# The first expert's tokens gathered alone, the group's other three behind its first products, and the table of Exp fetched in the projection

## The chip, the cores and the metric

The kernel runs on one NeuronCore of a Trainium2 chip, as one program in one launch. The metric is the device time of that launch in microseconds. Its engines work side by side, each through its own queue in order: TensorE (PE in the profile, with its weight loads listed apart as PEld), VectorE (DVE), ScalarE (ACT), GpSimd (POOL) and SyncE (SP), which here issues nearly all DMA transfers. TensorE's clock has two levels, 1.2 and 2.4 GHz; the profile shows which one was granted (PEclk 0.50 or 1.00).

## What is computed

Two layers of a hybrid backbone over 256 context and 256 latent tokens of 1024 features. In each layer a token mixer with four branches is followed by an expert-choice mixture of experts, and the change lies in the second of these and just ahead of it:

```python
def expert_choice_moe(h, router, w1, w3, w2):
    '''Each expert picks its top-C tokens of the routed set (one sample of one stream) by softmax affinity.'''
    B, L, D = h.shape
    cap = CAPACITY_FACTOR * L // N_EXPERTS
    aff = jax.nn.softmax((h @ router).astype(jnp.float32), axis=-1)
    g, idx = lax.top_k(aff.transpose(0, 2, 1), cap)
    xg = jax.vmap(lambda hb, ib: hb[ib])(h, idx)
    a = jnp.einsum('becd,edf->becf', xg, w1)
    b = jnp.einsum('becd,edf->becf', xg, w3)
    y = jnp.einsum('becf,efd->becd', jax.nn.silu(a) * b, w2) * g[..., None].astype(h.dtype)
    return jax.vmap(lambda yb, ib: jnp.zeros((L, D), h.dtype).at[ib.reshape(-1)].add(yb.reshape(-1, D)))(y, idx)
```

There are 16 experts of inner width 1024, each with three weight matrices of 4 MB in float32. Each expert takes 32 tokens of each stream. `h` is the normalised and modulated residual. Layer 0 routes two streams, context and latent; layer 1 routes the latent stream alone.

## The kernel before

Everything is float32. A float32 product of TensorE shows in the trace as two records, each with a weight load of its own. Time is split into a start, the mixer of layer 0 (to about 644 us), its expert stage (to about 1125), the mixer of layer 1 and its expert stage (from about 1535 to the end).

**The end of the mixer.** The last loop of `mixer` is the output projection: eight column blocks `wo0` to `wo7`, each a weight DMA, a split of the weights on ScalarE (L843) and VectorE (L844), products into a bank called `pd`, and a residual update on VectorE (L1421). After each block `pre.step(d)` of the class `MoePre` squares the new residual on ScalarE (L584) for the sums over tokens; after the last one `tokens` turns these sums, and the router's products, into columns by token.

**The start of the expert stage** (`moe`). VectorE computes a reciprocal root and the logits, ScalarE their Exp (L1454), VectorE the softmax. Then four rounds of maximum, replace and find index pick 32 tokens for each expert and stream (L1469 to L1473). Meanwhile `pre.transposes` turns the residual into rows by token, `xt`, through TensorE (L428) and copies on ScalarE (L674).

**The gather.** The experts go in four groups of four. `one_hot(gr)` builds, for the four experts of a group, a matrix OH of ones at the chosen tokens, scaled by the reciprocal root: one multiply on VectorE (L1571), one product with ones that spreads the rows over the partitions, and a comparison for each stream and half of the tokens (L1577). `gather(gr)` multiplies `xt` with OH, for each of eight feature blocks `k`, stream and half of the tokens one product with 128 x 128 weights out of `xt` and 128 moving columns (4 experts of 32 tokens). A bank `pm` holds two blocks in layer 0 and four in layer 1; there are two such banks in turn, and ScalarE (L1605) and VectorE (L1603) take them out with scale and shift into `xg`, in turns.

**The experts.** `ffn(e)` takes four weight tiles of 1 MB for w1 and four for w3 and multiplies the gathered tokens with them into two banks `pd`; ScalarE's Silu (L1636) and a multiply on VectorE (L1637) give the inner activations, TensorE transposes them (L1640), VectorE copies them (L1641), and the w2 products go into a bank `ps`. The group after next is gathered after the third expert of a group, and `scatter` adds the results to the residual after each group.

**Weights and queues.** A weight tile is fetched by SyncE into a slot (L1614) as soon as the slot's old contents have been read; before the expert stage begins some are already fetched, as slots come free. SyncE issues in order and waits at each slot. The order on the other engines is set by the scheduler from priorities in program order.

## Time and profile before

| | us |
|---|---|
| median of three runs (2004.29 to 2011.41) | 2009.74 |
| the profiled execution's own time | 2006.5 |
| its span in the trace | 2004.7 |
| TensorE busy in the span | 1843.2 (92%) |
| VectorE busy | 854.7 (43%) |
| ScalarE busy | 529.9 (26%) |
| mean DMA rate over the span | 274 GB/s |

A busy share is a mean over stages with different limits. To see what a change in one stage is worth, one goes to that stage: which engine is full there, what the others wait for, and whether a delay there is still seen at the stage's end. The times in the trace count from the start of the span. In the list of waits and in the chain, the line L431 is a helper through which nearly all products go, so one tells them apart by their tiles: `pm` for one-hot and gather, `pd` for the first products of an expert, `ps` for the rest.

### The profile page before, as it was taken

How to read it: one execution, taken by the hardware profiler on the slowest of the kernel's cores; microseconds unless marked ns; L12 is line 12 of the kernel's file. 1: busy time of each engine (PE TensorE's matmuls, PEld its weight loads, DVE VectorE, ACT ScalarE, POOL GpSimd, SP SyncE). 2: the span in 40 equal slices, each digit the busy share in tenths (PEclk: the TensorE clock that was granted, in tenths of full speed). 3: DMA queues.
4: the chain of work that ended last, by engine and by line, in shares of the span. 5: the costliest groups of instructions: out<-in, count | busy, mean ns of one | idle time of the engine just before them, and what ended most of it. 6: DMA issues, size and time to landing. Idle time of an engine off the chain costs nothing.

```text
span 2004.7 us, 28151 instructions
## 1 busy us (share of the span) xinstructions
PE 1843.2 (92%) x11524; PEld 1087.6 (54%) x11524; DVE 854.7 (43%) x1855; ACT 529.9 (26%) x932; POOL 27.9 (1%) x52
## 2 busy tenths in 40 slices
PE   7999999999999899999897799999998999987877
PEld 3667778877887443434232356788997333221213
DVE  5355658798743222221121345869865021110101
ACT  4433447522233110101000243447443000000000
POOL 0000000000000000000000010010000000000000
PEclk9989999999999899999999999999998999999999
DMA  8641122364545999999999855333578999999999
GB/s 312 223 140 58 64 85 78 107 236 136 194 156 218 353 399 350 387 409 409 409 409 409 302 189 180 117 106 137 200 262 336 409 409 409 409 409 409 409 409 332
DMA packets 154148, 550.07 MB, mean 274 GB/s; under 512 B 11042, under 2 KB 22690, under 8 KB 153124
## 3 DMA queue, kind: packets, MB, share of 16 engines
q1 hardware_dynamic: 153444, 545.13, 71.7%
q0 software_dynamic: 576, 3.15, 0.5%
q8 instruction: 91, 1.49, 0.3%
q14 instruction: 37, 0.30, 0.0%
HBM read 545.08 MB, written 3.15 MB: 273 GB/s over the span
## 4 chain that ended last, share of the span: by engine, by line
PE 69%; DMA 19%; DVE 7%; issue 3%; ACT 3%; SPq 0%; DVEq 0%; ACTq 0%
PE pd L431 40%; PE ps L431 15%; DMA base<-moe_w 8%; PE pm L431 7%; DMA r<-moe_w 6%; PE pa L431 4%; DMA base<-ada_w 2%; PE pm L428 1%; DMA base<-wg 1%; DVE base L527 1%; DVE r L844 1%; ACT r L843 1%; PE ps L1640 1%; DMA base<-cb 0%; DVE r L1236 0%
## 5 line engine op out<-in xcount | busy, mean ns | idle before, releaser
L431 PE MATMUL pd<-r 128*128 128x256 f32 (+3 forms) x2976 | 574.4, 364 | 12.9 <-DMA r<-moe_w 6.5
L431 PEld LDWEIGHTS pd<-r 128*128 128x128 f32 (+2 forms) x2976 | 427.3, 184 | 131.4 <-issue 53.8
L431 PE MATMUL pd<-r,r 128*128 128x512 f32 (+3 forms) x1304 | 282.6, 433 | 13.4 <-DMA r<-moe_w 10.8
L431 PEld LDWEIGHTS pd<-r,r 128*128 128x128 f32 (+2 forms) x1304 | 161.8, 166 | 105.0 <-issue 54.8
L844 DVE TENSOR_TENSOR r<-base,r 128x1024 fp32r<-128x1024 f32 x136 | 165.9, 1222 | 110.4 <-ACT r L843 110.0
L843 ACT ACTIVATE r<-base 128x1024 fp32r<-128x1024 f32 x136 | 143.4, 1058 | 252.2 <-PE pd L431 181.2
L431 PE MATMUL ps<-base 32*64 32x64 f32 (+12 forms) x2372 | 177.2, 279 | 15.1 <-DMA base<-hy 5.1
L431 PE MATMUL pd<-r,base 128*32 128x512 f32 (+1 forms) x680 | 166.5, 598 | 11.3 <-DMA r<-moe_w 10.6
L431 PEld LDWEIGHTS ps<-base 32*64 32x64 f32 (+7 forms) x2372 | 112.6, 142 | 76.3 <-issue 42.7
L431 PE MATMUL pm<-base 128*128 128x128 f32 (+12 forms) x660 | 106.1, 327 | 17.5 <-DVE base L1571 5.8
L431 PE MATMUL ps<-r,base 128*64 128x512 f32 (+4 forms) x468 | 98.6, 525 | 12.9 <-DVE base L1641 6.3
L431 PE MATMUL pd<-base 128*32 128x512 f32 (+1 forms) x408 | 100.5, 595 | 6.4 <-DMA base<-moe_w 5.6
L431 PEld LDWEIGHTS pm<-base 128*128 128x128 f32 (+5 forms) x660 | 72.8, 180 | 60.9 <-issue 33.6
L431 PEld LDWEIGHTS pd<-r,base 128*32 128x32 f32 (+1 forms) x680 | 42.0, 122 | 111.2 <-issue 76.4
L1637 DVE TENSOR_TENSOR r<-base,pd 64x512 f32<-64x512 f32 x16 | 10.9, 679 | 214.3 <-PE pd L431 214.3
L1637 DVE TENSOR_TENSOR base<-base,pd 128x512 f32<-128x512 f32 x16 | 11.0, 688 | 190.1 <-PE pd L431 155.9
L1636 ACT ACTIVATE base<-pd 128x512 f32<-128x512 f32 (+1 forms) x32 | 19.0, 594 | 251.1 <-PE pd L431 251.1
L431 PE MATMUL pa<-r,r 128*128 128x512 f32 (+1 forms) x384 | 82.4, 342 | 1.1 <-DVE base L905 1.1
L1687 ACT ACTIVATE base<-ps 32x512 f32<-32x512 f32 (+2 forms) x28 | 14.7, 525 | 251.6 <-PE ps L431 247.2
L1687 ACT ACTIVATE r<-ps 32x512 f32<-32x512 f32 (+2 forms) x32 | 15.3, 480 | 246.2 <-PE ps L431 240.3
L431 PE MATMUL pd<-base,r 128*32 128x512 f32 (+1 forms) x296 | 71.3, 597 | 9.3 <-DMA base<-moe_w 9.3
L1685 DVE COPY r<-ps 32x512 f32<-32x512 f32 (+2 forms) x32 | 17.8, 555 | 123.3 <-ACT r L1687 123.2
(246 smaller groups left out, 1728.8 us busy)
## 6 DMA issues: line engine op xcount, KB each, us to landing
r<-moe_w SPq DMA_DIRECT2D x251, 1024.0 KB, 18.1
base<-moe_w SPq DMA_DIRECT2D x131, 1024.0 KB, 17.4
base<-wg SPq DMA_DIRECT2D x152, 512.0 KB, 3.6
base<-ada_w SPq DMA_DIRECT2D x60, 512.0 KB, 4.7
base<-ada_t SPq DMA_DIRECT2D x24, 512.0 KB, 3.3
r<-ada_w SPq DMA_DIRECT2D x12, 512.0 KB, 10.2
base<-xT SPq DMA_DIRECT2D x4, 1024.0 KB, 6.8
filters<-r SPq DMA_DIRECT2D x8, 256.0 KB, 4.0
```

The costliest lines, as they stand in the source:

```text
L428: T.transpose(out, in_, ident)
L431: return T.matmul(out, lhsT, rhs, start=start, stop=stop, **kw)
L527: V.tensor_tensor_reduce(self.junk() if s == 0 else b(), b(), self.cb(s * 1024, n=1024), 1.0, cs("adab", l * 48 + c * 8 + j, n=1), OP.mult ...
L843: A.activation(w[0](), raw(), AF.Copy)
L844: V.tensor_tensor(w[1](), raw(), F(w[0]()), op=OP.subtract)
L1636: A.activation(s_(np_=rows), pa[0:rows, :], AF.Silu)
L1637: V.tensor_tensor(h_(np_=rows), s_(np_=rows), pb[0:rows, :], op=OP.mult)
L1640: T.transpose(p[:, q * rows:q * rows + rows], h_(q * 128, n=128, np_=rows), cs("ident", n=rows, np_=rows))
L1685: V.tensor_copy(dst, src)
L1687: A.activation(dst, src, AF.Copy)
```

## The change

Three things are changed in both layers.

First, `MoePre.step` issues an Exp of one column after the second block of the output projection, into a buffer that nobody reads.

Second, the first gather of a layer is made by a function of its own, `gather_one`, for expert 0 alone. Its one-hot has 32 columns for each stream and half; its products have 32 moving columns instead of 128 and all lie in one bank. The bank is taken out by VectorE alone, in two halves, by a multiply and an add for each.

Third, the other three experts of the first group are gathered by `gather(0, 1, 3)`, called in `ffn(0)` behind the products of w1 and w3. The one-hot now takes the first expert and the number of experts as arguments. The other three groups are gathered as before.

```diff
--- before.py
+++ after.py
@@ -659,6 +659,10 @@
 
         def step(self, k):
             self.sums.step(k)
+            if k == 1:
+                z = mem.take(8)
+                A.activation(z(n=1), self.sq[1](0, n=1), AF.Exp, scale=-1.0)
+                z.free()
             if k == KB - 1:
                 for b in self.sq + [self.AR]:
                     b.free()
@@ -1566,20 +1570,37 @@
                     else:
                         A.activation(dst, src, AF.Copy)
 
-        def one_hot(gr):
-
-            V.tensor_tensor(ge(0, [[128, NS], [32, 4], [1, 32]], np_=ne), gi(0, [[0, NS], [0, 4], [1, 32]], np_=ne),
-                            cs("sel", gr, [[4, NS], [8, 4], [0, 32]], np_=ne), op=OP.mult)
+        def one_hot(gr, j0, nj):
+
+            n = nj * 32
+            V.tensor_tensor(ge(0, [[n, NS], [32, nj], [1, 32]], np_=ne), gi(0, [[0, NS], [0, nj], [1, 32]], np_=ne),
+                            cs("sel", j0 * 8 + gr, [[4, NS], [8, nj], [0, 32]], np_=ne), op=OP.mult)
             p = ps("m")
-            mm(p[:, 0:NS * 128], cs("ones", np_=ne), ge(n=NS * 128, np_=ne), True, True)
+            mm(p[:, 0:NS * n], cs("ones", np_=ne), ge(n=NS * n, np_=ne), True, True)
             for s in range(NS):
                 for tb in range(2):
-                    V.tensor_scalar(OH((s * 2 + tb) * 128, n=128), p[:, s * 128:s * 128 + 128], cs("tok", tb, n=1),
+                    V.tensor_scalar(OH((s * 2 + tb) * 128 + j0 * 32, n=n), p[:, s * n:s * n + n], cs("tok", tb, n=1),
                                     rs(8 + tb * NS + s, n=1), op0=OP.is_equal, op1=OP.mult)
 
+        def gather_one(gr):
+
+            one_hot(gr, 0, 1)
+            x, p, n = xg[gr % 2], ps("m"), NS * CAP
+            for k in range(KB):
+                for s in range(NS):
+                    c = k * n + s * CAP
+                    for tb in range(2):
+                        mm(p[:, c:c + CAP], pre.xt((s * 2 + tb) * D + k * 128, n=128), OH((s * 2 + tb) * 128, n=CAP),
+                           tb == 0, tb == 1)
+            for k in range(0, KB, 4):
+                dst = x(k * 4 * nt, [[4 * nt, 4], [CAP, NS], [1, CAP]])
+                src = p[:, k * n:(k + 4) * n].rearrange("p (k s c) -> p k s c", s=NS, c=CAP)
+                cols = lambda b, o: b(o + k * 2 + 2 - NS, [[2, 4], [1, NS], [0, CAP]])
+                V.tensor_tensor(dst, src, cols(pre.Ac, 0), op=OP.mult)
+                V.tensor_tensor(dst, dst, cols(mod[l], 48), op=OP.add)
+
         def gather(gr, j0=0, nj=4):
-            if j0 == 0:
-                one_hot(gr)
+            one_hot(gr, j0, nj)
             x = xg[gr % 2]
             n = nj * 32
             per = min(KB, 512 // (NS * n))
@@ -1625,6 +1646,8 @@
                     for half in range(2):
                         mm(p[half * nt:half * nt + nt, :], x((k * 4 + j) * nt, n=nt),
                            w[k // 2]((k % 2) * 1024 + half * 512, n=512), k == 0, k == KB - 1)
+            if e == 0:
+                gather(0, 1, 3)
             read = w1 + w3
             n0 = len(slots)
             for b in read[::-1] if e == 0 else read:
@@ -1725,7 +1748,7 @@
             S.dma_start(out=cn(LATE + n_, n=CN.n - LATE - n_), in_=ins["cn"][:, LATE + n_:])
 
         nxt, spare = [], []
-        gather(0)
+        gather_one(0)
         for gr in range(4):
             for j in range(4):
                 ffn(4 * gr + j)
```

TensorE at the start of layer 0's expert stage, before, from behind the one-hot product on. `pm` 128x128 is the gather, `pd` the w1 and w3 products, the 128x128 of L1640 the transposes of the inner activations, and the last row the w2 products:

```order
L431 MATMUL pm_4971<-base 128x128 x8
L431 MATMUL pm_4984<-base 128x128 x8
L431 MATMUL pd_5031<-r_4867,base 64x512
L431 MATMUL pm_4997<-base 128x128 x8
L431 MATMUL pm_5010<-base 128x128 x8
L431 MATMUL pd_5031<-r_4867,base 64x512 x15
L431 MATMUL pd_5032<-r_4867,base 64x512 x8
L431 MATMUL pd_5032<-base 64x512 x8
L431 MATMUL pd_5106<-base 64x512
L1640 MATMUL ps_5067<-base 128x128 x4
L431 MATMUL pd_5106<-base 64x512 x2
L431 MATMUL ps_5077<-base 64x512 x16
```

The whole gather of four experts stands there ahead of all but one of expert 0's products. The same engine and place now, down to the last row ahead of the w2 products:

```order
L431 MATMUL pm_4972<-base 128x32 x32
L431 MATMUL pm_5052<-base 128x192
L431 MATMUL pd_5017<-r_4868,base 64x512 x16
L431 MATMUL pd_5018<-r_4868,base 64x512 x8
L431 MATMUL pd_5018<-base 64x512 x8
L431 MATMUL pm_5058<-base 128x96 x8
L431 MATMUL pm_5071<-base 128x96 x8
L1663 MATMUL ps_5112<-base 128x128 x3
L431 MATMUL pm_5084<-base 128x96 x8
L1663 MATMUL ps_5112<-base 128x128
L431 MATMUL pd_5151<-base 64x512
L431 MATMUL pm_5097<-base 128x96 x8
```

All 32 gather products of expert 0 now stand ahead of `pd`, with the 192-column one-hot product of the other three between; the other three's products, 96 columns each, stand between the w3 products and the w2 products of expert 0.

VectorE in that place, before:

```order
L1577 TENSOR_SCALAR base<-pm_4965,base 128x128 x4
L1571 TENSOR_TENSOR base<-base 32x256
L1603 TENSOR_SCALAR base<-pm_4971,base 128x4x32 x2
L1603 TENSOR_SCALAR base<-pm_4984,base 128x4x32 x2
L1603 TENSOR_SCALAR base<-pm_4997,base 128x4x32 x2
L1603 TENSOR_SCALAR base<-pm_5010,base 128x4x32 x2
L1637 TENSOR_TENSOR base<-base,pd_5032 128x512
```

The comparisons of 128 columns (L1577) and four banks' share of the evacuation (L1603) stand ahead of the multiply with Silu's result (L1637). VectorE in the same place now:

```order
L1576 TENSOR_TENSOR base<-base 32x64
L1582 TENSOR_SCALAR base<-pm_4966,base 128x32 x4
L1576 TENSOR_TENSOR base<-base 32x192
L1599 TENSOR_TENSOR base<-pm_4972,base 128x4x64 x2
L1600 TENSOR_TENSOR base<-base 128x4x64 x2
L1582 TENSOR_SCALAR base<-pm_5052,base 128x96 x4
L1576 TENSOR_TENSOR base<-base 32x256
L1660 TENSOR_TENSOR base<-base,pd_5018 128x512
L1624 TENSOR_SCALAR base<-pm_5058,base 128x3x32 x2
L1624 TENSOR_SCALAR base<-pm_5071,base 128x3x32 x2
```

Where ScalarE and VectorE took the gather out in turns, VectorE now takes expert 0's out by two multiplies and two adds ahead of the other three's comparisons.

ScalarE from the second block of the projection on, now; the table load before stood ahead of the Exp of L1454 (L1458 now), behind seven of the copies of `xt`:

```order
L847 ACTIVATE r_227<-base 128x1024
L584 ACTIVATE base<-base 128x512
L664 ACT_TABLE_LOAD
L664 ACTIVATE base<-base 128x1
L847 ACTIVATE r_227<-base 128x1024
L584 ACTIVATE base<-base 128x512
```

The load and the one-column Exp stand between the square of the second block and the split of a later one. No other table load was added on this engine.

## Rows read from the trace of the kernel before

**Rows 1.** Page, part 4: the chain that ended last, shares by engine.

```profile
PE 69%; DMA 19%; DVE 7%; issue 3%; ACT 3%; SPq 0%; DVEq 0%; ACTq 0%
```

**Rows 2.** Windows in layer 0's expert stage; the first line names the columns.

```profile
core 0: us, PE busy (x) PEld busy (x) DVE busy (x) ACT busy (x) POOL busy (x), PEclk, DMA share, GB/s
...
790.00:800.00 10.00, 10.00 (x48) 3.94 (x48) 1.74 (x4) 0.60 (x1) 0.00 (x0) 1.00 0.86 305
...
840.00:850.00 10.00, 10.00 (x50) 3.36 (x48) 1.38 (x2) 1.18 (x2) 0.00 (x0) 1.00 1.02 408
```

**Rows 3.** Waits of PE, 660 to 850: who, total us, times, longest.

```profile
PE ps L431 <- DVE base L1641: 3.8, 3, 2.7
```

**Rows 4.** DMA issues, 810 to 840: count, KB each, median us to landing.

```profile
r<-moe_w SPq DMA_DIRECT2D x9, 1024.0 KB, 6.8
```

**Rows 5.** Timeline, layer 0: start, length, engine, line, operation, [idle before].

```profile
647.71 2.56 ACT L674 ACTIVATE base<-ps 128x512 f32<-128x512 f32 x5 [1.10 <-PE ps L428]
...
650.28 1.28 ACT L1454 ACT_TABLE_LOAD   x1
...
658.66 0.41 DVE L1571 TENSOR_TENSOR base<-base 32x256 f32<-32x256 f32 x1
...
659.12 1.22 PE L431 MATMUL pm<-base 32*128 32x256 f32 x2 [5.84 <-DVE base L1571]
```

**Rows 6.** Chain of waits, same place: start, length, engine, tile, count.

```profile
660.85 6.09 PE pm L431 x32
...
666.94 1.00 PE pd L431 x2
...
667.94 3.77 PE pm L431 x32
...
671.71 7.03 PE pd L431 x31
...
685.68 0.70 DVE base L1637
...
686.43 0.66 PE ps L1640 x4
...
688.09 6.87 PE ps L431 x32
```

**Rows 7.** Timeline: records of one column with 128 x 128 weights.

```profile
26.68 2.59 PE L431 MATMUL ps<-base,r 128*128 128x1 f32 x14
...
645.76 1.45 PE L431 MATMUL pm<-base 128*128 128x1 f32 x12
```

**Rows 8.** Windows around those and the gather; PEclk is the granted clock.

```profile
26.00:27.00 1.00, 1.00 (x11) 0.57 (x10) 0.16 (x1) 0.00 (x0) 0.00 (x0) 1.00 1.04 414
...
27.00:28.00 1.00, 1.00 (x8) 1.00 (x8) 0.00 (x0) 0.00 (x0) 0.00 (x0) 0.66 1.01 406
...
28.00:29.00 1.00, 1.00 (x6) 1.00 (x6) 0.00 (x0) 0.00 (x0) 0.00 (x0) 0.50 1.04 414
...
664.00:666.00 2.00, 2.00 (x13) 2.00 (x13) 0.73 (x2) 0.48 (x2) 0.00 (x0) 0.60 1.02 410
```

**Rows 9.** Groups of one shape: a VectorE multiply of 256 columns from PSUM.

```profile
L1197 DVE TENSOR_TENSOR base<-pm,base 128x256 f32<-128x256 f32 x8 | 3.4, 423 | 2.0 <-PE pm L431 1.8
```

**Rows 10.** Timeline of ScalarE in the projection, with idle time before.

```profile
611.91 1.06 ACT L843 ACTIVATE r<-base 128x1024 fp32r<-128x1024 f32 x1 [3.72 <-DMA base<-wg]
```

**Rows 11.** Layer 1: chain of waits; landings issued 1530-1540, then 1570-1580.

```profile
1545.62 5.75 PE pm L431 x32
...
1551.38 13.88 PE pd L431 x64
...
1567.62 6.87 PE ps L431 x32
...
DMA to landing us min/median/max: 4.7/10.2/19.3
...
DMA to landing us min/median/max: 7.6/9.3/11.9
```

## The prediction

> **What bounds the kernel now.** I read the chain that ended last first, then the stretches of the two expert stages, then single rows. The chain is mostly TensorE, with DMA second [rows 1]. In the expert stage of layer 0 (660 to 1125 us) both hold it in turn: at 790 TensorE is full and the DMA engines have room (305 GB/s); at 840 they are full at 408 and stay so [rows 2]. From 660 to 850 the longest of TensorE's waits are for VectorE, 3.8 us in three times; it waits for no weight [rows 3]. A weight DMA is issued when a slot comes free, that is when TensorE has read the old contents; up to 840 it lands 6.8 us after issue [rows 4], hardly more than the 4.7 of an empty queue [rows 11], so the queue is waiting for slots. So whatever TensorE loses before about 830 makes every later weight land that much later, and the full queue behind cannot win it back. The expert stage of layer 1 is different: there the transfers are ahead, and a loss counts only as far as it exceeds their lead, 7.6 - 4.7 = 2.9 us where it is smallest [rows 11].
>
> At the start of the layer-0 stage there is a chain of its own: ScalarE copies, loads the table for Exp, VectorE picks the tokens (L1469 to L1473), then one-hot, its product and the gather [rows 5, 6]. TensorE stands still meanwhile and its granted clock is at half, 1.2 GHz, when the gather begins; within 664 to 666 it rises to 2.4 (mean 0.60, so at about 665.6) [rows 8].
>
> **The change, part by part (layer 0).**
>
> *Table of Exp.* The load takes 1.28 us, right behind the copies' end at 650.27 [rows 5], and Exp and all of VectorE's picking stand behind it. Without it Exp waits for a hand-over of some 0.14 from VectorE instead: 1.14 us gained. In its new place the load and the one-column Exp (1.5 us together) fall into ScalarE's idle time of 3.72 us ahead of the next weight split [rows 10]: cost nothing. Without that cover the split would be up to 1.5 us late, and TensorE has whole weight blocks in hand there. In layer 1 there was no load in this place: nothing gained.
>
> *One-hot for one expert.* Before: 658.66 to 660.85, 2.19 us [rows 5, 6]. Now 64 columns instead of 256: VectorE 0.2 (0.41 at 256 columns [rows 5]; between a quarter, 0.1, and the whole; I take the half), the product 0.53 (1.22 at 256 columns [rows 5]; a quarter of it, 0.31, and a fixed start of some 0.2), VectorE 0.2, three hand-overs 0.13: 1.06. It saves 1.13. The gather can start at 660.85 - 1.14 - 1.13 = 658.6.
>
> *The gather of one expert.* This is the term that decides. There are 32 products, 64 records, exactly as many as the whole gather had; only their moving columns fall from 128 to 32, while each still loads 128 x 128 weights of its own. What does a record cost when it moves few columns? The trace has no 32-column stream, but both sides of it. At full clock 32 records of 128 columns take 3.77 us, 0.118 each [rows 6]; 12 records of one column (four of them of 32) take 1.45, 0.121 each [rows 7]. So the price does not depend on the columns up to 128: the weights set it. At half clock, 14 one-column records from 26.68 on take 2.59 us [rows 7]; the clock falls at about 27.3 (mean 0.66 over 27 to 28 [rows 8]), 5.3 of them fit before that at 0.121, and the other 8.7 share the remaining 1.95 us less some 0.15 for the last one's end: about 0.208 each.
>
> Which clock? In the same stretch the clock stands at full over 26 to 27 and at half over 28 to 29 while TensorE is busy 1.00 throughout [rows 8]: weight loads with few columns do not hold it up. The 128-column gather did raise it. Thirty-two columns are a quarter of that activity, so I take it that the clock stays at half to the end of the one-expert gather: 64 x 0.208 = 13.3 us, to 671.9. The other bound is a rise at 665.6 as before: 7.0 us at half for 34 records, 30 x 0.118 = 3.6, to 669.2.
>
> The Trainium skill ("TensorE: Matmul & The Clock Gate", section "Part 1: The HAM clock gate") says that activity releases the throttle; what counts as activity it leaves open. By that sentence alone the packed gather would raise the clock as the old one did, which is the other bound.
>
> *Evacuation.* Before, four banks alternated and TensorE went on with the next bank. Now all 32 products write one bank, the first multiply on VectorE waits for all of them, and the order on VectorE is multiply, multiply, add, add; the first product of the expert needs the first add. That is 3 x 0.42 [rows 9] and a hand-over, 1.36 us, with only the 192-column one-hot product of the other three in TensorE's queue in it. So the expert's products start at 673.3 (other bound 670.5). Before, they ran from 671.71 with one product done at 666.94 [rows 6].
>
> *First products.* 32 products of 0.43 us, 13.8 us at full clock (the row at 671.71 to the multiply at 685.68 less the one product of the next expert [rows 6]). With the clock at half at first, I add 2 us (some 4 us at half; between 0 and 3): they end at 689.1 against 685.6 before.
>
> *The other three, behind them.* 64 records of 96 columns, again 0.118 each: 7.55 us. Before, TensorE idled and did transposes (0.66) and two products of the next expert in the 2.4 us from 685.68 to 688.09 [rows 6]; now it does 7.55 + 0.66 of transposes + 0.43 of one product = 8.64, since the next product (moe_w2 of expert 0) stands behind all four banks in TensorE's queue. It starts at 697.7, 9.6 us late, and two products of expert 1 (0.86) that were done before it are still to do: **10.5 us late** (other bound 5.8). Gone into it are 64 more records than before. ScalarE's load for Silu is covered by the first products.
>
> *Who waits.* The slots of expert 0's w1 and w3 come free some 3 us late, those of w2 and everything behind 10.5 us late; by the first paragraph all of this reaches the end of the stage.
>
> **Layer 1.** One stream instead of two: 32 records. The one-hot is some 0.7 shorter, the gather starts at 1544.9 instead of 1545.62 and takes 32 x 0.208 = 6.7, the evacuation 0.9 (half the columns, three operations of about 0.3): first products at 1552.6 against 1551.38 [rows 11], taking 13.9 and 2 more for the half clock; then 32 x 0.118 = 3.8 for the other three. The products end at 1568.5, and 3.8 for the three, the transposes and three products of the next expert (1.7) follow: the w2 products start at 1574.0 against 1567.62 [rows 11], 6.4 us late. The transfers' lead is 2.9 us, so 3.5 us reach the end (bounds 0, if the lead holds, and 6.4).
>
> **Sum.** 10.5 + 3.5 = 14.0 us. The profiled execution took 2006.5 us itself, so the sum gives 2020.5 against that; the median of the three runs is 2009.7, 3.2 above it, and 2009.7 + 14.0 = 2023.7 is the forecast.
>
> **The rivals.**
>
> *The clock rises as before.* For it: the gather of before raised it with the same number of records. Against: the one-column rows. Layer 0 then loses 5.8 us; in layer 1 the lag of 6.4 is shorter by 2.0 (products at full clock) and 0.8 (gather), and 0.7 of it shows: 2016.2.
>
> *Columns set the price (no slower at the end).* If a record of 32 columns cost a quarter of one of 128, the one-expert gather would take 64 x 0.052 = 3.4 us even at half clock, the first products would start at 663.4, and with 64 x 0.089 for the rest the w2 products would be 1.3 us early in layer 0: 2008.4. It decides as soon as a record of 32 columns costs less than about 0.06 us. Against it stands the row of one-column records at 0.121.
>
> The Trainium skill ("TensorE: Matmul & The Clock Gate", section "Back-to-back issue gap") gives an isolated gap that grows with the moving columns, which is this rival, and adds that with a weight load for each product both set the spacing; the trace bears out the second.
>
> *The transfers take the delay up.* If the queue of layer 0 turns out to have a lead before 830, only the late w1 and w3 slots (3 us) show, and layer 1 shows nothing: about 2012. Against: 305 GB/s at 790 and 6.8 us to landing.
>
> *It doesn't do what it says.* The load could still come ahead of Exp, or the three experts' products be drawn ahead of the first ones; then nothing would move, 2009.7. The order of the instructions shows neither, and it gets no chance of its own.
>
> **How the numbers follow.** Forecast case 0.60, at 2023.7, give or take 5 for the half-clock time of the products and layer 1's lead; clock as before 0.17 (2016.2); delay taken up 0.10 (2012); price by columns 0.08 (2008.4); a gain of more than that, which no row supports, 0.05. A measurement of this kernel tells about 0.5%, 10 us, from no change. Slower than 2019.8: most of the forecast case and a little of the second, 0.55; within 10 us: the rest of the forecast case, the second, third and fourth, 0.41; faster 0.04. The range from 2010 to 2030 leaves out the columns' case, the gain and the far end of the forecast case.
>
> **What would show it.** In the profile after: the one-expert gather as 64 records in 11 to 14 us, granted clock 0.50 throughout; 1.3 us between its end and the first product of pd; 64 records of 96 columns in 7.5 us behind pd; the first w2 product some 47 us after the Exp instead of 36.5; no table load ahead of Exp; the layer-0 stage longer by 10 us, that of layer 1 by 3 to 4. Wrong it would be if a record of 32 columns takes under 0.1 us at full clock, if the clock rises within the gather, or if TensorE in layer 0 waits for weights before 830.

## The result and the profile after

| | before | after |
|---|---|---|
| median of eight runs each, us | 2008.87 (2000.78 to 2011.41) | 2025.92 (2016.45 to 2029.46) |
| ratio after / before, 95% interval | | 1.0078 (1.0058 to 1.0098) |
| the profiled execution's span, us | 2004.7 | 2024.6 |

The changed kernel is slower by 0.78%, 15.7 us of 2008.87 (11.7 to 19.7 by the interval); the medians themselves differ by 17.05. The forecast was 14.0 us more and a time of 2023.7 in a range of 2010 to 2030. One execution of the run delay_l1s below (2121.13 us at a granted clock of 0.842) was in the slow state and is left out of its ratio.

To see in which stage the time went, I take as a marker the first step on VectorE behind the sum over tokens (L621 in all these kernels), which stands at the start of each expert stage and once in layer 1's mixer. Timeline rows of the kernel before, then of after (start, length, engine, line, operation, idle time before):

```profile
647.24 0.16 DVE L621 TENSOR_SCALAR base<-pm 128x4 f32<-128x4 f32 x1 [1.62 <-PE pm L431]
...
1149.51 0.16 DVE L621 TENSOR_SCALAR base<-pm 128x4 f32<-128x4 f32 x1 [0.87 <-PE pm L431]
...
1534.15 0.16 DVE L621 TENSOR_SCALAR base<-pm 128x2 f32<-128x2 f32 x1 [1.16 <-PE pm L431]
```

```profile
645.18 0.16 DVE L621 TENSOR_SCALAR base<-pm 128x4 f32<-128x4 f32 x1 [1.62 <-PE pm L431]
...
1159.73 0.16 DVE L621 TENSOR_SCALAR base<-pm 128x4 f32<-128x4 f32 x1 [0.87 <-PE pm L431]
...
1546.86 0.16 DVE L621 TENSOR_SCALAR base<-pm 128x2 f32<-128x2 f32 x1 [1.16 <-PE pm L431]
```

From the first marker to the second, which is the expert stage of layer 0 with the start of the mixer behind it, it is 514.6 us instead of 502.3 (+12.3); from the second to the third, the rest of layer 1's mixer, which the change doesn't touch, 387.1 instead of 384.6 (+2.5); from the third to the end 477.74 instead of 470.55 (+7.2). Up to the first marker it is 2.1 less. Some of this is scatter of single executions, so the experiments below are read as a set.

The head of layer 0's expert stage in the chain of waits of after (start, length, engine, tile, line, count), which answers to [rows 6]:

```profile
649.51 0.39 PE pm L428 x2
...
656.61 13.87 PE pm L431 x64
670.50 0.76 DVE base L1599 x2
671.26 0.34 DVE base L1600
671.65 15.45 PE pd L431 x64
687.09 3.74 PE pm L431 x32
...
695.99 7.02 PE ps L431 x32
```

The row at 656.61 is the gather of one expert: 64 records in 13.87 us, 0.217 each. Before, the gather of all four experts took 6.09 us for its first 32 records and 3.77 for the other 32 [rows 6], 9.86 in all. Behind it VectorE takes the bank out with TensorE waiting (1.15 us from 670.50 to 671.65), the first products take 15.45, the other three experts' gather follows from 687.09 on, and the w2 products start at 695.99. That is 50.8 us behind the marker, where before it was 688.09 - 647.24 = 40.9.

Windows of before, then of after in the same place, which answer to [rows 8] and [rows 2]. The last two columns are the share and the rate of the transfers (GB/s), the one ahead of them is TensorE's granted clock, and (x) is the number of records that touch the window:

```profile
670.00:672.00 2.00, 2.00 (x18) 1.72 (x18) 0.73 (x2) 1.13 (x3) 0.00 (x0) 1.00 0.03 10
...
674.00:676.00 2.00, 2.00 (x14) 0.59 (x10) 0.00 (x0) 0.77 (x1) 0.00 (x0) 1.00 0.54 154
...
692.00:700.00 8.00, 8.00 (x40) 2.58 (x38) 1.65 (x3) 1.39 (x3) 0.00 (x0) 1.00 1.01 396
```

```profile
656.00:658.00 2.00, 1.60 (x8) 1.41 (x8) 1.22 (x5) 0.00 (x0) 0.00 (x0) 0.50 1.03 412
...
664.00:666.00 2.00, 2.00 (x11) 2.00 (x11) 0.00 (x0) 0.00 (x0) 0.00 (x0) 0.50 1.03 412
...
670.00:672.00 2.00, 1.75 (x7) 1.12 (x8) 1.50 (x5) 0.00 (x0) 0.00 (x0) 0.50 0.00 0
...
674.00:676.00 2.00, 2.00 (x10) 0.66 (x8) 0.00 (x0) 0.00 (x0) 0.00 (x0) 0.83 0.00 0
...
692.00:700.00 8.00, 8.00 (x48) 4.36 (x48) 1.92 (x5) 2.15 (x5) 0.00 (x0) 1.00 0.13 31
...
790.00:800.00 10.00, 10.00 (x44) 5.48 (x43) 6.12 (x14) 0.07 (x1) 0.00 (x0) 1.00 0.78 276
...
840.00:850.00 10.00, 8.36 (x40) 2.77 (x38) 1.38 (x2) 0.00 (x0) 0.00 (x0) 1.00 1.02 413
```

Weight loads fill the gather (PEld 2.00 of 2.00), the clock is 0.50 throughout and rises only at about 674.7, within the first products. The rate falls to 0 twice: around 670, when every free slot is filled and TensorE hasn't yet read the first weights, and around 696, when the next slots wait for the late w2 products. From 645 to 705 SyncE's longest waits are 23.3 us for products into `pd` and 13.7 for products into `ps` (19.8 and 7.2 before). Before, the first of these gaps is there too, but shorter; the second isn't (396 GB/s against 31). At 840 the transfers are full again, as before. From 645 to 830 TensorE waits for no weight in either kernel; its longest waits are for VectorE.

The same in layer 1, chain of waits of after, which answers to [rows 11]:

```profile
1557.97 7.05 PE pm L431 x32
...
1565.79 15.50 PE pd L431 x64
1581.28 3.74 PE pm L431 x32
...
1586.82 0.03 PE ps L431
...
1587.25 6.44 PE ps L431 x30
```

The table of Exp: timeline of ScalarE of after, with [rows 5] and [rows 10] as the rows of before: the load stands in the projection, and nothing loads ahead of Exp at 648.38.

```profile
606.14 1.28 ACT L664 ACT_TABLE_LOAD   x1
...
609.80 1.06 ACT L847 ACTIVATE r<-base 128x1024 fp32r<-128x1024 f32 x1 [2.16 <-PE pd L431]
...
648.38 0.26 ACT L1458 ACTIVATE base<-base 128x64 f32<-128x64 f32 x1 [0.17 <-DVE base L1457]
```

### The profile page after: what moved, and what is told of

Same layout as the page of the kernel before. It is cut to its first block, busy times and chain, and to the rows that moved or that the text cites. A ratio compares the mean times of both kernels' runs of the same rounds, so it can differ in the third digit from the quotient of the medians.

```text
span 2024.6 us, 28369 instructions
## 1 busy us (share of the span) xinstructions
PE 1864.2 (92%) x11624; PEld 1105.2 (55%) x11624; DVE 857.8 (42%) x1871; ACT 529.5 (26%) x934; POOL 28.0 (1%) x52
## 4 chain that ended last, share of the span: by engine, by line
PE 69%; DMA 18%; DVE 7%; issue 3%; ACT 2%; SPq 1%; DVEq 0%; ACTq 0%
PE pd L431 40%; PE ps L431 15%; DMA r<-moe_w 9%; PE pm L431 7%; PE pa L431 5%; DMA base<-moe_w 5%; DMA base<-ada_w 2%; PE pm L428 1%; DVE base L527 1%; DMA base<-wg 1%; DVE r L848 1%; ACT r L847 1%; PE ps L1663 1%; SPq L1635 1%; DMA base<-ada_t 1%
## 5 line engine op out<-in xcount | busy, mean ns | idle before, releaser
L431 PE MATMUL pm<-base 128*128 128x128 f32 (+15 forms) x760 | 123.5, 328 | 17.7 <-issue 5.7
L431 PEld LDWEIGHTS pm<-base 128*128 128x128 f32 (+5 forms) x760 | 90.2, 193 | 61.5 <-issue 34.8
L1708 DVE COPY base<-ps 32x512 f32<-32x512 f32 (+2 forms) x28 | 17.1, 611 | 129.8 <-ACT base L1710 129.7
## 6 DMA issues: line engine op xcount, KB each, us to landing
r<-moe_w SPq DMA_DIRECT2D x251, 1024.0 KB, 18.1
base<-moe_w SPq DMA_DIRECT2D x131, 1024.0 KB, 18.1
r<-ada_w SPq DMA_DIRECT2D x12, 512.0 KB, 10.6
```

The source lines that it names most:

```text
L431: return T.matmul(out, lhsT, rhs, start=start, stop=stop, **kw)
L1708: V.tensor_copy(dst, src)
```

## The experiments

One table for all of them, one profiled execution each. "w2" is the start of the first w2 product behind the stage's marker. "Idle" is worked out from windows of 1 us, from 2 to 122 us behind the marker: the sum of what is missing to the full rate of 409 GB/s, in microseconds at that rate; where the windows begin changes it by some 0.2. The stage of layer 0 is taken with the mixer behind it, because the marker between them moves with TensorE while the transfers run through.

| kernel | w2, layer 0 | idle | stage + mixer | w2, layer 1 | idle | stage |
|---|---|---|---|---|---|---|
| before | 40.9 | 10.8 | 886.9 | 33.5 | 1.3 | 470.6 |
| after | 50.8 | 20.9 | 901.7 | 40.0 | 7.0 | 477.7 |
| exp_only | 38.7 | 8.4 | 889.1 | 34.3 | 1.5 | 472.1 |
| l0_only | 51.8 | 21.6 | 902.1 | 34.2 | 1.6 | 471.6 |
| l1_only | 38.8 | 8.3 | 887.8 | 40.0 | 7.5 | 477.6 |
| cols16 | 50.9 | 20.9 | 901.0 | 40.5 | 8.2 | 478.8 |
| wide | 47.7 | 17.8 | 893.7 | 38.5 | 6.0 | 475.3 |
| warm_after | 50.4 | 20.7 | 902.9 | 40.8 | 8.6 | 478.4 |
| warm_before | 37.0 | 7.0 | 886.1 | 33.2 | 1.1 | 470.6 |
| warm_l0 | 37.0 | 6.8 | 885.8 | 34.2 | 2.0 | 472.0 |
| delay_l0 | 51.5 | 19.1 | 898.3 | 33.2 | 1.2 | 470.6 |
| delay_l1 | 40.0 | 9.8 | 889.0 | 40.5 | 7.7 | 477.5 |
| delay_l1s | 40.3 | 9.9 | 891.2 | 37.9 | 5.3 | 475.4 |

Three of these have the same code as before up to layer 1's expert stage (before, delay_l1, delay_l1s): 886.9, 889.0 and 891.2 for layer 0's stage and mixer. So a single value there is good to some 4 us. The kernels were run in four sets, each with executions of before of its own, and a total is compared with those. In layer 1's stage the six kernels with neither split nor delay lie between 470.6 and 472.1.

### One part alone

exp_only is the changed kernel with the old call of the gather:

```diff
-            if e == 0:
-                gather(0, 1, 3)
...
-        gather_one(0)
+        gather(0)
```

> The kernel before with the one-column Exp alone; the gather is the old one. Theory (weights set the price of a product, all of the loss lies in the split gather): the Exp of the softmax of layer 0 finds its table there, 1.1 to 2 us earlier than before; nothing is lost anywhere else, and the two expert stages last as in before (502.3 and 470.6 us from the first step after the token sum to the next such step or the end). Total 1 to 2 us less, which is at the edge of what can be measured. Rival (the Exp in the projection is itself in the way, and a part of the 17 us lost comes from it): the total rises.

Measured: 2004.28 us against 2005.66, ratio 0.9994 (0.9979 to 1.0010). The softmax's transposes start 4.33 us behind the marker (645.32) instead of 5.46: 1.13 gained, as forecast (1.14). The w2 products are 2.2 earlier, since the clock happened to rise somewhat sooner as well (the first 32 records of the gather 5.28 instead of 6.09). The two stages take 500.2 and 472.1 us (502.3 and 470.6 before). In the total it can't be told from no change, and it isn't slower beyond 0.1%. The Exp isn't what costs.

l0_only and l1_only have the split in one layer; l1_only has (1,) in place of (0,):

```diff
-            if e == 0:
+            if e == 0 and l in (0,):
                 gather(0, 1, 3)
...
-        gather_one(0)
+        gather_one(0) if l in (0,) else gather(0)
```

> The changed kernel with the split gather in layer 0 alone; layer 1 gathers as before. Theory: layer 0's expert stage is 12 us longer as in the changed kernel (514.6 us), layer 1's is 470.6 us as in the kernel before; with the Exp's 1 to 2 us the total is 9 to 11 us above before, and 6 to 7 us below the changed kernel: the rest of the loss is layer 1's whole lag of 7 us. Rival (layer 1's transfers run ahead by about 3 us and take a part of the delay, as the prediction had it, and the rest of the 7.2 us was chance of one execution): the total is 13 to 14 us above before.

> The changed kernel with the split gather in layer 1 alone. Theory as mended (every microsecond by which the first w2 pass of layer 1 is late reaches the end): layer 1's expert stage is 6 to 8 us longer than before, the rest as in the kernel with the Exp alone; total 5 to 7 us above before. Theory as predicted (3.5 us reach the end): 2 to 3 us above.

Measured for layer 0 alone: 2019.11 us against 2005.66, ratio 1.0066 (1.0043 to 1.0090), 13.2 us more (8.6 to 18.1). That is nearer to the rival's total than to the theory's 9 to 11, and the interval holds both. The rows decide what the total can't: layer 1's stage is 471.6, as without the split, so the split in layer 1 is worth 477.7 - 471.6 = 6.1 in the changed kernel, not 3.5. What makes the total large is layer 0: with its mixer 902.1, against 889.1 with the Exp alone.

Measured for layer 1 alone: 2009.78 us against 2008.43, ratio 1.0015 (0.9996 to 1.0034). Its stage takes 477.6, which is 7.0 more than before, as the mended theory said of the stage, and 5.5 more than with the Exp alone; the total of 3 us more (-0.8 to 6.8) lies below the 5 to 7 expected of it and its interval holds both theories. I go by the stage, and by the delays below.

### What sets a record's price

cols16 moves half the columns, so that half of the first expert's tokens are left out; the bank is set to zero first (arguments shortened to ... here):

```diff
+  V.memset(p, 0.0)
...
-  mm(p[:, c:c + CAP], pre.xt(...), OH((s * 2 + tb) * 128, n=CAP), tb == 0, tb == 1)
+  mm(p[:, c:c + 16], pre.xt(...), OH((s * 2 + tb) * 128, n=16), tb == 0, tb == 1)
```

> The changed kernel with 16 columns moved instead of 32 in each record of the first expert's gather; half of the first expert's gathered tokens are left out (zeros stand in their place). Theory (the load of 128x128 weights sets the price, and the clock stays at half): the 64 records take 13.6 to 13.9 us in layer 0 and the 32 of layer 1 take 6.8 to 7.1, as with 32 columns. Rival (columns set the price): 7 us and 3.5 us.

Measured, chain of waits in layer 0 and in layer 1:

```profile
653.35 13.85 PE pm L431 x64
...
1554.26 7.02 PE pm L431 x32
```

13.85 and 7.02 with 16 columns, 13.87 and 7.05 with 32. Half of the columns changes nothing: at half clock a record costs 0.216 to 0.220 us with 16 columns as with 32. The rival on columns falls.

That the weights set the price, and not a fixed cost of every record, is seen where records have narrower weights. A row of before, with the granted clock at 1.00 over 502 to 504:

```profile
502.70 0.67 PE L431 MATMUL pm<-base 128*32 128x2 f32 x16
```

Sixteen records of two columns with weights of 128x32 take 0.67 us, 0.042 each. The one-column records with weights of 128x128 take 0.121 [rows 7].

### What the clock does under these records

warm_after puts six products of 512 columns, read by nobody, between the softmax's transposes and the one-hot's product:

```diff
-        V.tensor_copy(at[0](np_=ne), pa[0:ne, 0:256])
+        picked = V.tensor_copy(at[0](np_=ne), pa[0:ne, 0:256])
+        with tc.issue_after(picked.ins):
+            for _ in range((6, 6)[l]):
+                mm(pa, ident, cn(0, n=512), True, True)
```

> The changed kernel with six products of 512 columns, whose results nobody reads, put on TensorE between the softmax's transposes and the one-hot's, in both layers, so that TensorE works where it waited. Theory (each record costs its load of 128x128 weights, at the clock that is granted; half of the loss is the clock): if the clock is full when the gather begins, its 64 records take 7.6 us rather than 13.9, and if it stays full, the products behind it 13.9 rather than 15.5; the six products, 5.1 us at full clock and 10.2 at half, fill a wait of some 5 us, and what goes beyond it is lost. The expert stage of layer 0 is then 3 to 8 us shorter than in the changed kernel, that of layer 1 likewise. Rival (columns set the price): the gather takes under 4 us at full clock. Rival (the clock isn't what the gather waits for): 13.9 us stay at full clock.

Measured: 2025.15 us against 2005.66, ratio 1.0100 (1.0079 to 1.0120), no better than the changed kernel; the two stages take 514.3 and 478.4 us (514.6 and 477.7 in after) and are not 3 to 8 us shorter. Windows of layer 0, then its chain of waits:

```profile
654.00:656.00 2.00, 2.00 (x7) 0.76 (x5) 0.00 (x0) 0.00 (x0) 0.00 (x0) 1.00 1.01 406
656.00:658.00 2.00, 1.60 (x15) 1.46 (x14) 1.22 (x5) 0.00 (x0) 0.00 (x0) 1.00 1.04 414
658.00:660.00 2.00, 2.00 (x16) 2.00 (x15) 0.00 (x0) 0.00 (x0) 0.00 (x0) 0.76 1.02 406
660.00:662.00 2.00, 2.00 (x11) 2.00 (x11) 0.00 (x0) 0.00 (x0) 0.00 (x0) 0.50 1.04 416
...
670.00:672.00 2.00, 2.00 (x7) 0.47 (x4) 1.13 (x4) 0.00 (x0) 0.00 (x0) 0.50 0.00 0
```

```profile
656.56 11.66 PE pm L431 x64
...
669.38 15.57 PE pd L431 x64
```

The products did raise the clock: it is at 1.00, the level of 2.4 GHz, when the gather begins. Then it falls at about 659, with TensorE busy 2.00 of 2.00, and stays at 1.2 GHz into the first products, which take 15.57. So full clock served only some 2.5 microseconds of the gather. The same six products ahead of the old gather (warm_before) are the comparison: there the granted clock is 1.00 in every window from 652 to 668, as in this row from within its gather of 128 columns a record:

```profile
660.00:662.00 2.00, 2.00 (x19) 2.00 (x19) 0.29 (x2) 0.46 (x1) 0.00 (x0) 1.00 1.05 420
```

In layer 1 of warm_after most of the 32 records fit in before the clock fell (1.00 over 1560 to 1562, 0.89 over 1562 to 1564, so at about 1563.6, 0.50 behind). They take 4.07 us from 1560.25 on. The last 0.8 of it, at 0.217 a record, hold some 3.5 records; the other 28.5 share 3.3 us, about 0.116 each (an estimate). In warm_before 32 records of 128 columns take 3.93, 0.123 each, at 1.00 throughout. So at full clock, too, a record of 32 columns costs about what one of 128 columns costs.

Nothing was gained in the end. The six products outlast the wait that they fill, so the gather starts 13.1 us behind the marker instead of 11.4 in layer 0, and 13.9 instead of 11.1 in layer 1; and the first products behind it still begin at half clock (15.57 and 16.54 us). My expectation had a condition, "if the clock stays full", and the condition failed.

wide moves the one-hot columns of all four experts in each of the 64 records, at overlapping places of the same bank, so that the first expert's tokens are wrong; the number of records and their weights are those of the changed kernel (arguments shortened to ... here):

```diff
             one_hot(gr, 0, 1)
+            one_hot(gr, 1, 3)
...
-                    c = k * n + s * CAP
+                    w = min(k * n + s * CAP, 384)
...
-  mm(p[:, c:c + CAP], pre.xt(...), OH((s * 2 + tb) * 128, n=CAP), tb == 0, tb == 1)
+  mm(p[:, w:w + 128], pre.xt(...), OH((s * 2 + tb) * 128, n=128), tb == 0, tb == 1)
```

> The changed kernel, in which each record of the first expert's gather moves 128 columns (the one-hot columns of all four experts, whose second product and comparisons stand ahead as well) instead of 32, into the same bank at overlapping places, so that the first expert's gathered tokens are wrong; number and weights of the 64 records are as in the changed kernel. Theory (the clock stays at half under records of 32 columns, as it fell there from full in the kernel with the six products ahead; with 128 columns it rises as in the kernel before): the clock rises within the gather, which takes 8 to 11 us rather than 13.9, and the first w1 and w3 passes that follow take 13.9 rather than 15.5. Rival (the clock goes by the time since TensorE's last wait, whatever it moves): it stays at 0.50 through the gather and the gather takes 13.9 us or more.

Measured: windows and chain of waits in layer 0.

```profile
656.00:658.00 2.00, 2.00 (x12) 2.00 (x11) 0.10 (x1) 0.00 (x0) 0.00 (x0) 0.50 1.03 408
658.00:660.00 2.00, 2.00 (x11) 2.00 (x11) 0.00 (x0) 0.00 (x0) 0.00 (x0) 0.50 1.03 408
660.00:662.00 2.00, 2.00 (x19) 2.00 (x19) 0.00 (x0) 0.00 (x0) 0.00 (x0) 0.97 1.00 401
```

```profile
655.05 9.84 PE pm L431 x64
...
666.05 13.95 PE pd L431 x64
```

Four times the columns, and the gather is 4.0 us shorter; the first products behind it are 1.5 us shorter. The count (x) of records in 2 us goes from 11 to 19 as the clock rises at about 660. In layer 1 the 32 records take 5.35 instead of 7.05 and the first products 13.93 instead of 15.50. The rival that the clock goes by the time since TensorE's last wait falls: the rise comes 5.1 us behind that wait, and in after none came in 13.87 us. This kernel's only execution took 2012.06 us, which says little of its total; its w2 products are some 3 us earlier in layer 0 and 1.5 in layer 1 than in after, although a second one-hot stands ahead of its gather.

### Doing the same to the kernel before

warm_before has the six products of warm_after in both layers, the early Exp and the old gather; warm_l0 has them in layer 0 alone.

> The kernel before with the one-column Exp and with six products of 512 columns, whose results nobody reads, between the softmax's transposes and the one-hot's, in both layers; the gather is the old one, all four experts in one bank. Theory (the clock at the head of the gather costs time in the kernel before as well): its first 32 records take 3.8 us rather than 6.1 in layer 0, and 2 us less in layer 1; with the Exp 3 to 5 us are gained in all, less what the six products take beyond the wait that they fill (none to 5 us). Rival (the clock falls again before the one-hot, or the transfers of the weights set the pace anyway): the total stays at before, or rises by what the six products add.

> The kernel before with the one-column Exp, and the six products that keep the clock up ahead of the gather in layer 0 alone. Theory (in layer 0 the transfers stand still until the first pass frees a buffer, so that what the gather gains there reaches the end; in layer 1 they don't stand still, so that nothing is to be gained there, and the six products of layer 1 only came 1.3 us too long): 2 to 4 us less than before. Rival (what is gained at the head is lost to later waits of the same stage): no difference from before.

Measured: 2003.27 us against 2005.66, ratio 0.9989 (0.9975 to 1.0003), and 2004.79 against 2008.43, ratio 0.9990 (0.9972 to 1.0007). With them the first 32 records of layer 0's gather take 4.12 us (warm_before) instead of 6.09, the w2 products come 3.8 us earlier than in before and the transfers are idle some 4 us less. Layer 0's stage with its mixer takes 886.1 and 885.8, 2 to 3 less than exp_only and l1_only (889.1, 887.8), which is within the scatter of single values. Both medians lie 2 to 4 us below before, in the direction expected, and neither interval leaves out no change. I can't call either faster.

### The delay by itself

These are the kernel before (no Exp, no split) with products of 512 columns behind the first expert's h: twelve in layer 0 (10.57 us in the chain of waits), or eight (7.13) or four (3.70) in layer 1, which is 0.86 us for each further one.

```diff
             V.tensor_tensor(h_(np_=rows), s_(np_=rows), pb[0:rows, :], op=OP.mult)
+            if e == 0:
+                for _ in range((12, 0)[l]):
+                    mm(pb, ident, cn(0, n=512), True, True)
```

> The kernel before, with twelve products of 512 columns whose results nobody reads behind the first expert's h in layer 0: the w2 pass of the first expert comes 10.2 us later (12 x 0.853 us), nothing else is changed, there is no split gather and no early Exp. Theory (in layer 0 the transfers stand still for buffers, so that any lag of the first w2 pass goes to the stage's end whole): layer 0's expert stage and the total are 9.5 to 10.5 us longer. Rival (a part of the changed kernel's 12.3 us in layer 0 comes from something other than the lag, as from transfers disturbed by the split): the delay alone costs clearly less than it lasts, 7 us or under.

> The kernel before, with eight products of 512 columns whose results nobody reads behind the first expert's h in layer 1: the w2 pass there is 6.8 us late, about as in the changed kernel (6.9). Theory as mended (the transfers of layer 1 have hardly any lead): layer 1's expert stage is 6 to 7 us longer. Theory as predicted (a lead of 2.9 us): 3.5 to 4 us longer. Rival (layer 1's passes had taken the delay whole, and the changed kernel lost its time in the gather's own transfers): under 2 us.

> As the run before, with four products: the w2 pass of layer 1 is 3.4 us late. Theory as mended: layer 1's expert stage is 2.5 to 3.4 us longer. Theory as predicted (a lead of 2.9 us takes nearly all of it): 0.5 us longer or less. The difference between this run and the one with eight products tells a lead (the first microseconds are free, the next ones cost all) from a share (each microsecond costs a part).

Measured: in layer 0 the w2 products are 10.6 us later than in before, and the total is 2014.59 against 2005.72, ratio 1.0046 (1.0030 to 1.0063), 9.2 us more (6.0 to 12.6). The stage alone is only 3.8 longer than in before, not 9.5 or more; the mixer behind it is 7.5 longer. So the place at which I expected it was wrong. The sum of both is 898.3, against a mean of 889.0 for the three kernels that are the same up to there: 9.3, most of the delay.

In layer 1 I compare with the means of the six kernels without split or delay there, 33.8 for w2 and 471.2 for the stage. In delay_l1 w2 is 6.7 us later and the stage 6.3 longer (477.5); in delay_l1s w2 is 4.1 later, of which 0.8 (against before) is lost ahead of the four products, and the stage 4.2 longer (475.4). Their idle times say the same, 7.7 and 5.3 against 1.3 in before: 6.4 and 4.0. The totals, 1.0030 (1.0005 to 1.0054) and 1.0031 (1.0011 to 1.0051), agree with both and tell nothing finer. A lead of 2.9 us would have left 3.8 and 1.2 us; that is excluded. Less than one microsecond of the lag is free. Whether that is a small lead or a share of about a tenth, these two runs can't tell.

Where the lead went is to be seen in the windows of delay_l1s, with its marker at 1538.63:

```profile
1575.00:1576.00 1.00, 1.00 (x9) 0.47 (x8) 0.40 (x1) 0.00 (x0) 0.00 (x0) 1.00 1.05 418
1576.00:1577.00 1.00, 1.00 (x8) 0.34 (x6) 0.03 (x1) 0.00 (x0) 0.00 (x0) 1.00 0.16 61
1577.00:1578.00 1.00, 1.00 (x6) 0.23 (x4) 0.00 (x0) 0.00 (x0) 0.00 (x0) 1.00 0.10 33
1578.00:1579.00 1.00, 1.00 (x8) 0.28 (x6) 0.00 (x0) 0.00 (x0) 0.00 (x0) 1.00 0.00 0
1579.00:1580.00 1.00, 1.00 (x8) 0.30 (x6) 0.00 (x0) 0.00 (x0) 0.00 (x0) 1.00 0.72 78
1580.00:1581.00 1.00, 1.00 (x6) 0.23 (x4) 0.00 (x0) 0.00 (x0) 0.00 (x0) 1.00 0.90 324
1581.00:1582.00 1.00, 1.00 (x8) 0.28 (x6) 0.00 (x0) 0.00 (x0) 0.00 (x0) 1.00 1.04 430
```

and in SyncE's timeline, first of delay_l1s, then of before (issues of weights, time from the first to the last, count):

```profile
1578.31 3.80 SPq L1631 DMA_DIRECT2D r<-moe_w  x3
```

```profile
1569.39 3.80 SPq L1614 DMA_DIRECT2D r<-moe_w  x3
```

The queue of weights has run empty at about 1576.1, 37.5 us behind the marker (some 33 GB/s still move in the microsecond after). The next issue, for the first slot that the w2 products free, comes 1.8 us behind their start in both kernels: at 39.7 here, at 35.2 in before. Behind the issue at 1578.31 some 1.7 us are lost before the rate is full (0.7 in the rest of the first microsecond, 0.8 in the next, 0.2 in the third). If the queue of before would have run empty at the same distance from the marker, this transfer was issued 2.3 us ahead of that there, and 1.7 of these went into its start: a lead of about 0.6 us, an estimate from these rows.

## Why the prediction was right, and where it wasn't

**The gather of one expert** was the term that decides, and it was right in its mechanism and nearly in its size. Forecast: 64 records, 0.208 each, clock at half to the end, 13.3 us. Measured: 13.87, 0.217 each. The row it was drawn from, one-column records [rows 7], gave the price although no stream of 32 columns stood in the trace of before, and cols16 (16 against 32 columns at half clock) and the pair of warm_after and warm_before (32 against 128 at full clock) show that columns don't enter up to 128. The rise of the clock as before, the rival with 0.17, didn't come. None of the three signs of being wrong appeared: a record of 32 columns at full clock costs about 0.116 us, the clock didn't rise within the gather, and TensorE in layer 0 waits for no weight before 830.

The Trainium skill ("TensorE: Matmul & The Clock Gate", section "Part 1: The HAM clock gate") says that sustained activity releases the throttle. In warm_after the clock fell from 1.00 to 0.50 at about 659 while TensorE was busy 2.00 of 2.00 us, and in wide it rose at about 660 with the same records moving more columns. The measurement decides: what the profile calls busy is not enough to read the clock from.

**Exp** gained 1.13 (forecast 1.14). **The one-hot** for one expert: 656.61 - 655.25 = 1.36 us instead of 2.19, a gain of 0.83 (forecast 1.13; its product took 0.69 instead of 0.53, whose fixed start of 0.2 no row had shown). **Evacuation**: 1.15 us (forecast 1.36). **First products**: 15.45 (forecast 13.8 + 2). **The other three**: 3.74 + 1.76 + 1.95 = 7.45 us in the chain (forecast 7.55). The w2 products start 9.9 us late against the marker (forecast 9.6, and 10.5 with two products of expert 1 still to do). Each of these terms was good to about half a microsecond.

**Who waits, layer 0**: as far as can be told, all of it reaches the end. The four kernels with the split in layer 0 and 32 columns or fewer take 901.0 to 902.9 for stage and mixer (mean 901.9), against 889.0 of the three without split and Exp: 12.9 with a scatter of some 4, for a lag of 10.6 (mean w2 of 51.0 against 40.4); delay_l0 gives 9.3 for 11.1. The idle time of the transfers grows by 10.8 us in the four and by 8.9 in delay_l0. So the step holds. Whether the two microseconds above the lag are more than scatter stays open.

**Layer 1 is the step that failed**, as a term of the sum that was mis-sized: the part of the lag that the transfers take up. The lag was forecast at 6.4 us and is 6.5; "the transfers' lead is 2.9 us, so 3.5 us reach the end" is wrong. The split costs 478.1 (mean of four) - 471.2 (mean of six) = 6.9 us there, just above 6.4, the upper one of my own bounds. As far as these rows tell, none of the lag was taken up. I took the lead as the difference of two landing times, 7.6 in the stage less 4.7 at its start [rows 11]. The 7.6 belongs to the issue at 1571.11, the second of the group whose first is at 1569.39; SyncE's timeline of before has it as the first row here, and the landing of this issue alone is the second:

```profile
1571.11 0.37 SPq L1614 DMA_DIRECT2D r<-moe_w  x1
...
DMA to landing us min/median/max: 7.6/7.6/7.6
```

A transfer of 1 MB takes 2.6 us at 409 GB/s, so what it waited for beyond an empty queue was mostly the group's own first transfer, which the lag moves along with it, and not older transfers that would have bridged it. The first issue had only the 0.6 us worked out above.

With 6.9 in place of 3.5 the sum would have been 17.4 and the time 2027, against 2025.92. With the measured 15.7 (11.7 to 19.7) both sums stand within the interval. That the forecast's total came out within 2.3 us is therefore no test of this term; the stage rows, not the totals, tell the two apart.

**What the change was worth**: the early first gather saves no TensorE work ahead of the first products, since the weights of 64 records are loaded for one expert as for four, and then the same 64 once more for the other three. The half clock weighs as much: 64 records at the full-clock price of 0.118 [rows 6] would take 7.55 us instead of 13.87, and the products behind them 13.95 (wide) instead of 15.45, so that by this estimate some 7.8 us hang on the clock (2.3 hung on it in the kernel before, 6.09 - 3.77 in the first half of its gather). TensorE is busy 1864.2 us in the whole span instead of 1843.2, with 100 records more (64 and 32 of the gathers, 4 of the one-hots).

## What to carry to other kernels

Before splitting a product to get its first part sooner, count weight loads, not columns: a part with fewer moving columns and the same stationary blocks costs as much as the whole, here about 0.12 us a record at full clock and 0.217 at half, and the rest then pays it again. Read the clock too: a stretch that loads much and moves little can hold TensorE at 1.2 GHz though it is busy throughout (here for 13.87 us), and the work behind it starts there. A lead of transfers is read from when the queue would run dry against when the first late transfer is issued and begins to move, not from landing times within a group of issues.

## What had not been expected of the hardware

The clock fell within a busy stream of the expert stage too, as the prediction had read it from the one-column records [rows 8]: in warm_after from 1.00 to 0.50 at about 659, some 2.5 us into records of 32 columns, PE 2.00 of 2.00 in the window; moving four times the columns made the same 64 records faster (9.84 us against 13.87). A weight transfer of 1 MB issued into an empty queue lost about 1.7 us before the rate was full (delay_l1s, windows from 1578).
